# Transposes on the DMA queue in place of TensorE, in a two-group stream step

## The chip, the cores and the metric

One core of a Trainium2 chip runs the whole program. The metric is device time in microseconds of one execution, the median of three runs. TensorE (PE) multiplies, VectorE (DVE) and ScalarE (ACT) work element by element, GpSimd (POOL) and SyncE (SP) mostly start transfers, which 16 DMA engines carry out.

## The reference

One layer of an encoder for 256 prompt positions and 64 sample positions (320 columns in all, T), width 2048, float32.

```python
proj = rmsnorm(x, norm_mix) @ w_in           # q | k | v | u | vs | gates
# attention, 8 heads of 128; for the sample positions 256 cached keys and values stand ahead
z = (q @ k.T) * 128 ** -0.5
log_stay = where(mask, log_sigmoid(-z), 0)
log_rest = reverse_cumsum(log_stay) - log_stay
w = where(mask, exp(log_sigmoid(z) + log_rest), 0)
a = w @ v
# gating, 8 groups of 128 channels, chunks of 128 positions
u, vs = gelu(u), rmsnorm(gelu(vs), sgu_norm)
bb = u * (w_spatial_masked @ vs + b_spatial)
merged = sigmoid(g_a) * (a @ w_branch_a) + sigmoid(g_b) * (bb @ w_branch_b)
h = x + merged @ w_out
h = h + (silu(hn @ w_gate) * (hn @ w_up)) @ w_down     # hn = rmsnorm(h, norm_ffn), 5632 wide
y = rmsnorm(h, norm_final)
```

Outputs are y, k, v and the normalised vs rows of the sample.

## The kernel before

Features lie on the 128 partitions, the 320 positions along the free dimension. Nearly all work is projections: `block` multiplies one 128-column block of a weight with an activation in 16 chunks, in two half-blocks of 8. For each half-block `weights` loads 512 KB on SP's queue into a ring of three (`wraw`, tag `raw`), ScalarE rounds it to `wh` (line 75), VectorE takes the difference `wl` (line 76), both in rings of four (`wsplit`), and TensorE runs three matmuls a chunk (lines 83 to 85). A half-block is a tick: after each, `tick` emits what `at(tick, fn, ...)` has put there. So the attention and the gating branch lie between half-blocks of the projections of later heads. The framework's scheduler decides how each engine's instructions stand from this order and the dependencies; transfers under `keep_in_program_order` keep theirs.

Attention goes by pairs of heads (p = 0 to 3). `head_out` puts q, k, v into SBUF. `att_scores` multiplies q and k on TensorE and computes the weights on VectorE and ScalarE: `z[0]` and `z[1]` hold in the end the exponentials for the prompt (three 128 x 128 blocks a head), `z[0]` also two blocks for the cached rows, `wown` the sample's own block. `att_turn` transposes them and the values on TensorE, through `aux` banks of PSUM, from which ScalarE and VectorE copy to `wt` and `av`; `att_out` multiplies. `att_keys` and `att_rows` load cached keys and values (`cv`, one buffer). For each pair of gating groups `sgu_gain` scales `vs` (the sample's rows to `vown`), `sgu_turn` transposes five blocks on TensorE, `sgu_mix` multiplies with `wst` and `wso`. A transpose there is a matmul with the identity, `ident`.

`pair(name)` takes a 128 x 640 float32 buffer from a ring of eight, tag "D". After the branches follow the gates with the merge, the output projection and the feed-forward network, from about 330 us to the end; they are projections alone.

Of the kernel before, what the change touches and what calls it, by code (L numbers as in the profile page):

```python
# [8 lines left out]
F32 = mybir.dt.float32  # L9
# [4 lines left out]
P = 128  # L14
TP = 256
TS = 64
T = TP + TS
D = 2048
KD = D // P
H = 8  # L20
# [13 lines left out]
def stream_step(ctx: ExitStack, tc: tile.TileContext, xT, w_in, w_a, w_b, w_out, w_gu, w_down,  # L34
                gains, ws_t, bs, ck_t, cv, y_t, k_t, v_t, sv_t):
    nc = tc.nc
# [21 lines left out]
    def at(tick, fn, *a):  # L58
        assert tick > state["tick"], (tick, state["tick"])
        later.setdefault(tick, []).append((fn, a))  # L60
# [41 lines left out]
    def pair(name):  # L102
        return big.tile([P, 2 * T], F32, tag="D", bufs=8, name=name)
# [36 lines left out]
    ident = const.tile([P, P], F32, name="ident")  # L140
# [142 lines left out]
    attn = {}  # L283
    att_ctx = ExitStack()
    apool = att_ctx.enter_context(tc.tile_pool(name="attn", bufs=1))
# [21 lines left out]
    Z, KT = 384, T + PAST  # L307
# [7 lines left out]
    wown = apool.tile([P, P], F32, name="wown")  # L315
    nc.gpsimd.memset(wown, 0.0)
    ROWS = (slice(0, TS), slice(TS, P))
# [3 lines left out]
    def att_new(p):  # L321
        attn[p] = {"q": apool.tile([P, 2, T], F32, tag="q", bufs=2, name="q"),
                   "k": apool.tile([P, 2, KT], F32, tag="k", bufs=2, name="k"),
                   "v": apool.tile([P, 2, T], F32, tag="v", bufs=2, name="v"),
                   "vo": apool.tile([P, P], F32, tag="vo", name="vo")}

    def att_keys(p):
        tc.keep_in_program_order(nc.sync.dma_start(
# [44 lines left out]
        for r in ROWS:  # L373
            nc.scalar.activation(out=wown[r, r], in_=z[1][r, Z:], func=AF.Exp)

    def att_turn(p):

        s = attn[p]
        z, v = s["z"], s["v"]
        ba, bb, bs_, bv = aux(), aux(), aux(), aux()  # L380
        cols = lambda t, i: t[:, i * P : (i + 1) * P]
        for i in range(4):
            nc.tensor.transpose(cols(bv, i), v[:, i // 2, i % 2 * P : (i % 2 + 1) * P], ident)  # L383
        nc.tensor.transpose(cols(ba, 3), s["vo"], ident)
        for j, b in enumerate((ba, bb)):
            for i in range(3):
                nc.tensor.transpose(cols(b, i), cols(z[j], i), ident)  # L387
        for i in range(2):
            nc.tensor.transpose(cols(bs_, i), cols(z[0], 3 + i), ident)
        nc.tensor.transpose(cols(bs_, 2), wown, ident)  # L390
        wt = s["wt"] = apool.tile([P, 3 * Z], F32, tag="wt", name="wt")
        av = s["av"] = apool.tile([P, 5 * P], F32, tag="av", name="av")
        nc.scalar.copy(out=av[:, 0 : 4 * P], in_=bv)
        nc.vector.tensor_copy(wt[:, 0:Z], ba[:, 0:Z])
        nc.vector.tensor_copy(av[:, 4 * P :], ba[:, Z:])
        nc.scalar.copy(out=wt[:, Z : 2 * Z], in_=bb[:, 0:Z])
        nc.scalar.copy(out=wt[:, 2 * Z :], in_=bs_[:, 0:Z])

    def att_out(p):
        s = attn.pop(p)  # L400
        wt, av, cvt = s["wt"], s["av"], s["cv"]
        po = aux1(), aux()
        mm = lambda out, a, b, first, last: nc.tensor.matmul(out, a, b, start=first, stop=last, skip_group_check=True)  # L403

        mm(po[0][:, TP : TP + P], av[:, 4 * P :], wt[:, 2 * Z + 2 * P :], True, False)
        for j, r in enumerate(ROWS):
            for i in range(2):
                lo = 2 * Z + i * P + j * TS
                mm(po[0][:, TP + j * TS : TP + (j + 1) * TS], cvt[:, i, j, :], wt[:, lo : lo + TS], False, i == 1)
        for j in range(2):  # L410
            mm(po[j][:, 0:TP], av[:, 2 * j * P : (2 * j + 1) * P], wt[:, j * Z : j * Z + TP], True, False)
            mm(po[j][:, P:TP], av[:, (2 * j + 1) * P : (2 * j + 2) * P], wt[:, j * Z + TP : (j + 1) * Z], False, True)
        aT[2 * p] = split("B", po[0][:, 0:T])
        hi, lo = aT[2 * p + 1] = slot("B"), slot("B")
        for r, src in ((slice(0, TP), po[1][:, 0:TP]), (slice(TP, T), po[0][:, T : T + TS])):
            nc.scalar.copy(out=hi[:, r], in_=src)
            nc.vector.tensor_tensor(out=lo[:, r], in0=src, in1=hi[:, r].bitcast(F32), op=ALU.subtract)
# [3 lines left out]
    def head_out(name, ps, h):  # L421
        s = attn[h // 2]
        o = s[name][:, h % 2, 0:T]
        if name == "q":
            nc.vector.scalar_tensor_tensor(out=o, in0=ps, scalar=QSCALE, in1=got["rx"],
                                           op0=ALU.mult, op1=ALU.mult)
        else:
            nc.vector.tensor_tensor(out=o, in0=ps, in1=got["rx"], op=ALU.mult)
            nc.gpsimd.dma_start(out=(k_t if name == "k" else v_t)[h], in_=o)
        if name == "v":  # L430
            nc.gpsimd.tensor_copy(s["vo"][:, ROWS[h % 2]], o[:, TP:T])

    def first_out():
        for name, b in (("q", 0), ("k", 1), ("v", 2)):
# [2 lines left out]

    def attend(p, now):
        at(now + 2, att_scores, p)
        at(now + 4, att_rows, p)  # L440
        at(now + 10, att_turn, p)
        at(now + 14, att_out, p)

    att_new(0)
    at(state["tick"] + 1, first_out)
# [15 lines left out]
    vs, _ = halves(H, "vs")  # L461
    for g in range(H):
        ps = block(w_in[4 * H + g], xs)
        t = t320("ev")
# [3 lines left out]

    us, _ = halves(H, "us")
    bT: dict[int, tuple] = {}  # L470
    vown, vnat = {}, {}

    def sgu_norm():
        got["rv"] = rms("rv", [sq.total], H * P)
        sgu_gain(0)

    def sgu_gain(p):

        own = vown[p] = apool.tile([P, 2, T], F32, tag="q", bufs=2, name="vown")[:, 0, 0:P]
        for j in range(2):  # L480
            g = 2 * p + j
            for out, r in ((vs[g][:, 0:TP], slice(0, TP)), (own[:, j * TS : (j + 1) * TS], slice(TP, T))):
                nc.vector.scalar_tensor_tensor(out=out, in0=vs[g][:, r], scalar=g_sgu[:, g : g + 1],
                                               in1=got["rv"][:, r], op0=ALU.mult, op1=ALU.mult)
            nc.gpsimd.dma_start(out=sv_t[g], in_=own[:, j * TS : (j + 1) * TS])

    def sgu_turn(p):
        pt, po = aux(), aux()
        for i in range(4):
            nc.tensor.transpose(pt[:, i * P : (i + 1) * P], vs[2 * p + i // 2][:, i % 2 * P : (i % 2 + 1) * P], ident)  # L490
        nc.tensor.transpose(po[:, 0:P], vown.pop(p), ident)
        t = apool.tile([P, 5 * P], F32, tag="av", name="vsn") if p % 2 else apool.tile([P, 3 * Z], F32, tag="wt", name="vsn")
        vn = vnat[p] = t[:, 0 : 5 * P].rearrange("p (i d) -> p i d", i=5)
        nc.scalar.copy(out=vn[:, 0:4].rearrange("p i d -> p (i d)"), in_=pt)
        nc.scalar.copy(out=vn[:, 4], in_=po[:, 0:P])
        if p + 1 < H // 2:
            sgu_gain(p + 1)

    def sgu_mix(p):
        vn = vnat.pop(p)  # L500
        pg = [aux(), aux()]

        nc.tensor.matmul(pg[0][:, 256:384], vn[:, 4], wso[:, p], start=True, stop=True)
        for i in range(4):
            nc.tensor.matmul(pg[i // 2][:, i % 2 * P : (i % 2 + 1) * P], vn[:, i], wst[:, 2 * p + i // 2, :],  # L505
                             start=True, stop=True)
        for j in range(2):
            g = 2 * p + j
            b = t320("bb")
            nc.vector.tensor_tensor(out=b[:, 0:TP].rearrange("p (i t) -> p i t", i=2),  # L510
                                    in0=pg[j][:, 0:TP].rearrange("p (i t) -> p i t", i=2),
                                    in1=bsb[:, g : g + 1, :].broadcast_to([P, 2, P]), op=ALU.add)
            nc.vector.tensor_tensor(out=b[:, TP:T], in0=pg[0][:, TP + j * TS : TP + (j + 1) * TS],
                                    in1=bsb[:, g, 0:TS], op=ALU.add)
            nc.vector.tensor_tensor(out=b, in0=b, in1=us[g], op=ALU.mult)
            bT[g] = split("B", b)

    def sgu_both(p):
        if p:
            sgu_mix(p - 1)  # L520
        if p < H // 2:
            sgu_turn(p)

    base = state["tick"]
    at(base + 1, sgu_norm)
    for p in range(H // 2 + 1):
        at(base + 4 * p + 2 + (p == 0), sgu_both, p)
    for g in range(H):
        ps = block(w_in[3 * H + g], xs)
        t = t320("ev")  # L530
# [6 lines left out]
    for m in range(KD):  # L537
        gate = []
        for i in range(2):
            ps = block(w_in[5 * H + i * KD + m], xs)  # L540
            t = t320("ev")
# [8 lines left out]
        t = t320("mg", 1)  # L550
# [5 lines left out]
        lo = mpool.tile([P, T], F32R, tag="C", bufs=32, name="ml")  # L556
# [72 lines left out]
    ms, r = (const.tile([P, 3], F32, name=f"col{i}") for i in range(2))  # L629
# [9 lines left out]
    for n in (1, 1, 2, 2, 2, 2, 2, 2, 1, 1):  # L639
        y = ypair[done // 2].rearrange("p (c t) -> p c t", c=2)[:, done % 2 : done % 2 + n, :]  # L640
# [57 lines left out]
```

## Time and profile before

| what | value |
|---|---|
| runs | 1717.07, 1718.59, 1718.68 us, median 1718.59 |
| profiled execution | 1716.78 us, its span 1715.0 us |
| granted TensorE clock | 0.998 |
| busy: PE, DVE, ACT, POOL | 1702.2, 861.9, 658.8, 46.1 us |
| DMA | 263.32 MB, mean 154 GB/s |
| from 60 to 330 us (both branches) | DVE 150.6, ACT 133.6 us busy of 270, DMA share 0.46 |

The span is the time between the first and the last instruction on the core; the rest of the execution, 1.8 us, lies around it. Durations of matmuls in the profile overlap, since they are pipelined: what one costs is read from the starts of those that follow each other.

### The profile page before, as it was taken

Reading aid. Unit: us, or ns where it says so; the run is one execution under the profiler, and the core shown is the slowest. Engines: PE = TensorE matmul, PEld = TensorE weight load, DVE = VectorE, ACT = ScalarE, POOL = GpSimd, SP = SyncE. Lnnn points to the kernel's source line nnn. Section 1 sums busy time; section 2 is a strip of 40 time slices with the busy share of each in tenths; the row PEclk is TensorE's granted clock in tenths of the full one; section 3 lists DMA queues with packets and bytes.
Section 4 is the critical chain, followed back from the end, with each engine's and each line's share of the span. In section 5 each row is a group of like instructions: output and inputs, shape, how many; then the busy total and the mean of one; then the engine's idle time right before and its main releaser. Section 6 shows DMA issues by size and latency. Waiting matters only on the chain.

```text
span 1715.0 us, 27450 instructions
## 1 busy us (share of the span) xinstructions
PE 1702.2 (99%) x11616; PEld 1696.7 (99%) x11616; DVE 861.9 (50%) x1097; ACT 658.8 (38%) x819; POOL 46.1 (3%) x73
## 2 busy tenths in 40 slices
PE   9999999999999999999999999999999999999997
PEld 9999999999999999999999999999999999999997
DVE  7655446544444445555444444444444444444454
ACT  6454454433333333444333332233333323333332
POOL 0100011000000000110000000000000000000000
PEclk9999999999999999999999999999999999999999
DMA  7554444444444445554444445444444444444453
GB/s 260 162 193 143 144 154 145 139 148 148 149 153 152 148 152 165 174 171 149 150 148 148 150 152 153 148 148 148 152 151 152 148 148 150 151 153 149 130 150 114
DMA packets 80331, 263.32 MB, mean 154 GB/s; under 512 B 9008, under 2 KB 15408, under 8 KB 80208
## 3 DMA queue, kind: packets, MB, share of 16 engines
q1 hardware_dynamic: 78704, 258.25, 46.6%
q0 software_dynamic: 1088, 3.02, 0.5%
q8 instruction: 91, 1.49, 0.3%
q10 hardware_dynamic: 416, 0.31, 0.1%
q14 instruction: 32, 0.26, 0.0%
HBM read 256.03 MB, written 5.51 MB: 152 GB/s over the span
## 4 chain that ended last, share of the span: by engine, by line
issue 54%; PE 45%; DVE 0%; DMA 0%; ACT 0%; POOL 0%; POOLq 0%; ACTq 0%; DVEq 0%
PE acc L83 13%; PE acc L84 13%; PE acc L85 13%; PE aux L219 2%; PE acc L219 1%; PE aux L403 1%; DVE h L637 0%; DMA raw<-w_in 0%; PE aux L505 0%; PE aux L343 0%; PE aux L345 0%; PE aux L387 0%; PE aux L342 0%; PE aux L490 0%; PE aux L383 0%
## 5 line engine op out<-in xcount | busy, mean ns | idle before, releaser
L75 ACT CAST wh<-raw 128x1024 fp32r<-128x1024 f32 x468 | 484.5, 1036 | 988.0 <-PE acc L84 796.3
L76 DVE TENSOR_TENSOR wl<-raw,wh 128x1024 fp32r<-128x1024 f32 x468 | 564.2, 1206 | 506.4 <-ACT wh L75 503.9
L83 PE MATMUL acc<-A,wh 128*128 128x320 f32 x2464 | 763.1, 310 | 0.0
L85 PE MATMUL acc<-A,wl 128*128 128x320 f32 x2464 | 761.5, 309 | 0.0
L84 PE MATMUL acc<-A,wh 128*128 128x320 f32 x2464 | 761.4, 309 | 0.0
L83 PEld LDWEIGHTS acc<-A,wh 128*128 128x128 f32 x2464 | 462.6, 188 | 2.1 <-issue 2.0
L84 PEld LDWEIGHTS acc<-A,wh 128*128 128x128 f32 x2464 | 462.6, 188 | 0.2
L85 PEld LDWEIGHTS acc<-A,wl 128*128 128x128 f32 x2464 | 462.6, 188 | 0.0
L85 PE MATMUL acc<-B,wl 128*128 128x320 f32 x960 | 296.6, 309 | 0.0
L83 PE MATMUL acc<-B,wh 128*128 128x320 f32 x960 | 296.6, 309 | 0.0
L84 PE MATMUL acc<-B,wh 128*128 128x320 f32 x960 | 296.6, 309 | 0.0
L83 PEld LDWEIGHTS acc<-B,wh 128*128 128x128 f32 x960 | 180.2, 188 | 0.0
L84 PEld LDWEIGHTS acc<-B,wh 128*128 128x128 f32 x960 | 180.2, 188 | 0.0
L85 PEld LDWEIGHTS acc<-B,wl 128*128 128x128 f32 x960 | 180.2, 188 | 0.0
L83 PE MATMUL acc<-mh,wh 128*128 128x320 f32 x256 | 79.1, 309 | 0.0
L84 PE MATMUL acc<-ml,wh 128*128 128x320 f32 x256 | 79.1, 309 | 0.0
L85 PE MATMUL acc<-mh,wl 128*128 128x320 f32 x256 | 79.1, 309 | 0.0
L597 DVE TENSOR_TENSOR bb<-acc,rh 128x320 f32<-128x320 f32 x44 | 21.6, 491 | 57.8 <-PE acc L85 57.8
L594 DVE TENSOR_TENSOR ev<-acc,rh 128x320 f32<-128x320 f32 x44 | 21.6, 491 | 56.4 <-PE acc L85 56.3
L83 PEld LDWEIGHTS acc<-mh,wh 128*128 128x128 f32 x256 | 48.0, 188 | 0.0
L84 PEld LDWEIGHTS acc<-ml,wh 128*128 128x128 f32 x256 | 48.0, 188 | 0.0
L85 PEld LDWEIGHTS acc<-mh,wl 128*128 128x128 f32 x256 | 48.0, 188 | 0.0
(173 smaller groups left out, 696.2 us busy)
## 6 DMA issues: line engine op xcount, KB each, us to landing
raw<-w_gu SPq DMA_DIRECT2D x176, 512.0 KB, 3.5
raw<-w_in SPq DMA_DIRECT2D x141, 512.0 KB, 3.6
raw<-w_down SPq DMA_DIRECT2D x80, 512.0 KB, 3.5
raw<-w_out SPq DMA_DIRECT2D x32, 512.0 KB, 3.6
raw<-w_a SPq DMA_DIRECT2D x16, 512.0 KB, 3.5
raw<-w_b SPq DMA_DIRECT2D x16, 512.0 KB, 3.5
raw<-w_down SPq DMA_DIRECT2D x16, 256.0 KB, 2.7
xr<-xT SPq DMA_DIRECT2D x16, 160.0 KB, 2.6
```

What stands on the lines that cost most here:

```text
L75: nc.scalar.copy(out=wh[:, : n * P], in_=raw[:, : n * P])
L76: nc.vector.tensor_tensor(out=wl[:, : n * P], in0=raw[:, : n * P], in1=wh[:, : n * P].bitcast(F32), op=ALU.subtract)
L83: nc.tensor.matmul(ps[:, :T], a, x[0], start=first, stop=False)
L84: nc.tensor.matmul(ps[:, :T], a, x[1], start=False, stop=False)
L85: nc.tensor.matmul(ps[:, :T], b, x[0], start=False, stop=last)
L219: nc.tensor.matmul(first[b][h][:, :T], w[:, (h * n + j) * P : (h * n + j + 1) * P], xs[c + j][i], start=not last and c + j + i == 0, stop= ...
L403: mm = lambda out, a, b, first, last: nc.tensor.matmul(out, a, b, start=first, stop=last, skip_group_check=True)
L594: nc.vector.tensor_tensor(out=t, in0=pg, in1=got["rh"], op=ALU.mult)
L597: nc.vector.tensor_tensor(out=u, in0=pu, in1=got["rh"], op=ALU.mult)
```

## The change

The 32-bit words to be transposed are taken apart into two planes of 16 bits on ScalarE (`apart`, line 334), the low halves in one plane and the high halves in the other. One transposing DMA on SP's queue turns all 128 x 128 blocks of both planes (`turn`, line 340), and VectorE joins them to words again (`together`, line 345). This replaces the identity matmuls of `att_turn` and `sgu_turn` with their copies out of PSUM. Per pair of heads there are three such DMAs: the values (`vp`, 10 blocks of 16 bits), and the weights in two (`wp`, 10 and 8 blocks); per pair of gating groups one (`vsp`, 10 blocks). GpSimd's copies of `vo` go. The ticks move: `att_rows` from 4 to 11 after the pair's start, the turns to 6 and 12, the joins to 8 and 14, `att_out` from 14 to 16; in the gating branch each pair has a tick of its own for gain, turn, join and mix.

```diff
-                   "vo": apool.tile([P, P], F32, tag="vo", name="vo")}
+    def planes(name, n):
+        return pair(name)[:, 0:n].bitcast(U16).rearrange("p (w n) -> p n w", w=2)
+
+    def apart(to, src):
+        nc.scalar.copy(out=to, in_=src.bitcast(U16).rearrange("p (n w) -> p n w", w=2))
+
+    def turn(src):
+        n = src.shape[1]
+        to = planes("turned", n)
+        flat = lambda t: t.rearrange("p n w -> p w n").rearrange("p w n -> p (w n)")
+        tc.keep_in_program_order(nc.sync.dma_start(
+            out=flat(to).rearrange("p (b r) -> p b r", r=P), in_=flat(src), transpose=True))
+        return to
+
+    def together(to, src):
+        nc.vector.tensor_copy(to.bitcast(U16).rearrange("p (n w) -> p w n", w=2), src.rearrange("p n w -> p w n"))
...
+        y = s["wp"] = planes("wp0", 5 * P), planes("wp1", 4 * P)
+        apart(y[0], z[0])
+        apart(y[1][:, 0:Z], z[1][:, 0:Z])
+        apart(y[1][:, Z:], wown)
+    def att_turn(p, what):
         s = attn[p]
-        for i in range(4):
-            nc.tensor.transpose(cols(bv, i), v[:, i // 2, i % 2 * P : (i % 2 + 1) * P], ident)
-        nc.tensor.transpose(cols(ba, 3), s["vo"], ident)
-        for j, b in enumerate((ba, bb)):
-            for i in range(3):
-                nc.tensor.transpose(cols(b, i), cols(z[j], i), ident)
-        for i in range(2):
-            nc.tensor.transpose(cols(bs_, i), cols(z[0], 3 + i), ident)
-        nc.tensor.transpose(cols(bs_, 2), wown, ident)
...
+        s[what] = [turn(t) for t in ((s["vp"],) if what == "vt" else s["wp"])]
+
+    def att_join(p, what):
+        s = attn[p]
+        t = s[what]
+        if what == "vt":
+            av = s["av"] = apool.tile([P, 5 * P], F32, tag="av", name="av")
+            together(av, t[0])
+        else:
+            wt = s["wt"] = apool.tile([P, 9 * P], F32, tag="wt", name="wt")
+            together(wt[:, 0 : 5 * P], t[0])
+            together(wt[:, 5 * P :], t[1])
...
         if name == "v":
-            nc.gpsimd.tensor_copy(s["vo"][:, ROWS[h % 2]], o[:, TP:T])
+            j = h % 2
+            if j == 0:
+                s["vp"] = planes("vp", 5 * P)
+            apart(s["vp"][:, j * TP : (j + 1) * TP], o[:, 0:TP])
+            apart(s["vp"][:, 4 * P + j * TS : 4 * P + (j + 1) * TS], o[:, TP:T])
...
         at(now + 2, att_scores, p)
-        at(now + 4, att_rows, p)
-        at(now + 10, att_turn, p)
-        at(now + 14, att_out, p)
+        at(now + 6, att_turn, p, "vt")
+        at(now + 11, att_rows, p)
+        at(now + 8, att_join, p, "vt")
+        at(now + 12, att_turn, p, "wt")
+        at(now + 14, att_join, p, "wt")
+        at(now + 16, att_out, p)
...
     def sgu_turn(p):
-        pt, po = aux(), aux()
-        for i in range(4):
-            nc.tensor.transpose(pt[:, i * P : (i + 1) * P], vs[2 * p + i // 2][:, i % 2 * P : (i % 2 + 1) * P], ident)
-        nc.tensor.transpose(po[:, 0:P], vown.pop(p), ident)
...
+        vturned[p] = turn(vplane.pop(p))
...
-    for p in range(H // 2 + 1):
-        at(base + 4 * p + 2 + (p == 0), sgu_both, p)
+    for p, mix in enumerate((9, 11, 14, 18)):
+        at(base + 1 + 3 * p, sgu_gain, p)
+        at(base + 6 + 3 * p, sgu_turn, p)
+        at(base + (8, 10, 13, 16)[p], sgu_join, p)
+        at(base + mix, sgu_mix, p)
```

How the order moves is shown for pair 1 of the heads. First SP's queue, before: weight loads (`raw`) with the cached rows and keys of pairs 1 and 2 between them.

```order
L70 DMA raw<-w_in 128x1024 x5
L334 DMA cv<-cv 128x2x256
L70 DMA raw<-w_in 128x1024 x2
L328 DMA k<-ck_t 128x2x256
L70 DMA raw<-w_in 128x1024 x9
```

The same place after:

```order
L70 DMA raw<-w_in 128x1024 x6
L340 DMA_TRANSPOSE turned<-vp 128x10x128
L70 DMA raw<-w_in 128x1024
L354 DMA cv<-cv 128x2x256
L348 DMA k<-ck_t 128x2x256
L70 DMA raw<-w_in 128x1024
L340 DMA_TRANSPOSE turned<-wp_1186 128x10x128
L340 DMA_TRANSPOSE turned<-wp_1187 128x8x128
L70 DMA raw<-w_in 128x1024 x10
```

Three transposing DMAs have come in among the loads, with two loads between the first and the second. Each weight load waits for the split three half-blocks before it. Now VectorE, shortly after its last operation on the weights of pair 1, before (`wl` are the weight splits, `q`, `k`, `v` the heads of pair 2):

```order
L76 TENSOR_TENSOR wl<-raw,wh 128x1024 x2
L428 TENSOR_TENSOR v<-acc,rx 128x320
L76 TENSOR_TENSOR wl<-raw,wh 128x1024 x2
L428 TENSOR_TENSOR k<-acc,rx 128x320
L76 TENSOR_TENSOR wl<-raw,wh 128x1024 x2
L425 SCALAR_TENSOR_TENSOR q<-acc,rx 128x320
L76 TENSOR_TENSOR wl<-raw,wh 128x1024
L394 COPY wt<-aux 128x384
L395 COPY av<-aux 128x128
L76 TENSOR_TENSOR wl<-raw,wh 128x1024
```

The same after, where `B` are the results of pair 0:

```order
L76 TENSOR_TENSOR wl<-raw,wh 128x1024 x3
L448 TENSOR_TENSOR v<-acc,rx 128x320
L76 TENSOR_TENSOR wl<-raw,wh 128x1024
L118 TENSOR_TENSOR B<-aux_1320,B 128x320
L437 TENSOR_TENSOR B<-aux,B 128x256
L437 TENSOR_TENSOR B<-aux_1320,B 128x64
L345 COPY av<-turned 128x2x640
L76 TENSOR_TENSOR wl<-raw,wh 128x1024
L345 COPY wt<-turned 128x2x640
L345 COPY wt<-turned 128x2x512
L448 TENSOR_TENSOR k<-acc,rx 128x320
L76 TENSOR_TENSOR wl<-raw,wh 128x1024 x2
```

The copies out of PSUM, behind eight splits of weights, have become three joins behind four and five, and each join stands ahead of the splits that follow.

On ScalarE the words of `wp` are taken apart right after the exponentials of pair 1:

```order
L75 CAST wh<-raw 128x1024 x2
L392 ACT_TABLE_LOAD
L392 ACTIVATE z_1157<-z_1157 128x384
L394 ACTIVATE wown<-z_1157 64x64 x2
L391 ACTIVATE z_1156<-z_1156 128x640
L334 COPY wp_1186<-z_1156 128x640x2
L334 COPY wp_1187<-z_1157 128x384x2
L334 COPY wp_1187<-wown 128x128x2
L75 CAST wh<-raw 128x1024 x2
L334 COPY vp<-v 128x256x2
```

These three copies of `wp` now stand ahead of the next two casts of weights.

More of the change, by code (lines that the diff above doesn't have):

```diff
@@ L323, in att_new @@
                    "k": apool.tile([P, 2, KT], F32, tag="k", bufs=2, name="k"),
-                   "v": apool.tile([P, 2, T], F32, tag="v", bufs=2, name="v"),
-                   "vo": apool.tile([P, P], F32, tag="vo", name="vo")}
+                   "v": apool.tile([P, 2, T], F32, tag="v", bufs=2, name="v")}
+    U16 = mybir.dt.uint16
+    def planes(name, n):
[11 more added lines that the diff above has]
+        nc.vector.tensor_copy(to.bitcast(U16).rearrange("p (n w) -> p w n", w=2), src.rearrange("p n w -> p w n"))
     def att_keys(p):
@@ L374, in att_scores @@
             nc.scalar.activation(out=wown[r, r], in_=z[1][r, Z:], func=AF.Exp)
-    def att_turn(p):
-        s = attn[p]
-        z, v = s["z"], s["v"]
-        ba, bb, bs_, bv = aux(), aux(), aux(), aux()
-        cols = lambda t, i: t[:, i * P : (i + 1) * P]
-        for i in range(4):
-            nc.tensor.transpose(cols(bv, i), v[:, i // 2, i % 2 * P : (i % 2 + 1) * P], ident)
-        nc.tensor.transpose(cols(ba, 3), s["vo"], ident)
-        for j, b in enumerate((ba, bb)):
-            for i in range(3):
-                nc.tensor.transpose(cols(b, i), cols(z[j], i), ident)
-        for i in range(2):
[L389 to L397, printed above, removed]
+        y = s["wp"] = planes("wp0", 5 * P), planes("wp1", 4 * P)
[3 more added lines that the diff above has]
+    def att_turn(p, what):
+        s = attn[p]
+        s[what] = [turn(t) for t in ((s["vp"],) if what == "vt" else s["wp"])]
[9 more added lines that the diff above has]
+            together(wt[:, 5 * P :], t[1])
     def att_out(p):
@@ L403, in att_out @@
         mm = lambda out, a, b, first, last: nc.tensor.matmul(out, a, b, start=first, stop=last, skip_group_check=True)
-        mm(po[0][:, TP : TP + P], av[:, 4 * P :], wt[:, 2 * Z + 2 * P :], True, False)
+        mm(po[0][:, TP : TP + P], av[:, 4 * P :], wt[:, 8 * P :], True, False)
         for j, r in enumerate(ROWS):
             for i in range(2):
-                lo = 2 * Z + i * P + j * TS
+                lo = Z + i * P + j * TS
                 mm(po[0][:, TP + j * TS : TP + (j + 1) * TS], cvt[:, i, j, :], wt[:, lo : lo + TS], False, i == 1)
         for j in range(2):
-            mm(po[j][:, 0:TP], av[:, 2 * j * P : (2 * j + 1) * P], wt[:, j * Z : j * Z + TP], True, False)
-            mm(po[j][:, P:TP], av[:, (2 * j + 1) * P : (2 * j + 2) * P], wt[:, j * Z + TP : (j + 1) * Z], False, True)
+            w = wt[:, j * 5 * P : j * 5 * P + Z]
+            mm(po[j][:, 0:TP], av[:, 2 * j * P : (2 * j + 1) * P], w[:, 0:TP], True, False)
+            mm(po[j][:, P:TP], av[:, (2 * j + 1) * P : (2 * j + 2) * P], w[:, TP:], False, True)
         aT[2 * p] = split("B", po[0][:, 0:T])
@@ L470, in stream_step @@
     bT: dict[int, tuple] = {}
-    vown, vnat = {}, {}
+    vplane, vturned, vnat = {}, {}, {}
     def sgu_norm():
         got["rv"] = rms("rv", [sq.total], H * P)
-        sgu_gain(0)
     def sgu_gain(p):
-        own = vown[p] = apool.tile([P, 2, T], F32, tag="q", bufs=2, name="vown")[:, 0, 0:P]
+        own = apool.tile([P, 2, T], F32, tag="q", bufs=2, name="vown")[:, 0, 0:P]
         for j in range(2):
@@ L485, in sgu_gain, with sgu_join @@
             nc.gpsimd.dma_start(out=sv_t[g], in_=own[:, j * TS : (j + 1) * TS])
+        y = vplane[p] = planes("vsp", 5 * P)
+        for j in range(2):
+            apart(y[:, j * TP : (j + 1) * TP], vs[2 * p + j][:, 0:TP])
+        apart(y[:, 4 * P :], own)
     def sgu_turn(p):
-        pt, po = aux(), aux()
-        for i in range(4):
[L490 to L497, printed above, removed]
+        vturned[p] = turn(vplane.pop(p))
+    def sgu_join(p):
+        t = apool.tile([P, 5 * P], F32, tag="av", name="vsn") if p % 2 else apool.tile([P, 9 * P], F32, tag="wt", name="vsn")
+        together(t[:, 0 : 5 * P], vturned.pop(p))
+        vnat[p] = t[:, 0 : 5 * P].rearrange("p (i d) -> p i d", i=5)
     def sgu_mix(p):
@@ L516, in sgu_mix @@
             bT[g] = split("B", b)
[L518 to L522, printed above, removed]
     base = state["tick"]
     at(base + 1, sgu_norm)
-    for p in range(H // 2 + 1):
-        at(base + 4 * p + 2 + (p == 0), sgu_both, p)
+    for p, mix in enumerate((9, 11, 14, 18)):
[3 more added lines that the diff above has]
+        at(base + mix, sgu_mix, p)
     for g in range(H):
```

## The prediction

> **What bounds the kernel now.** The page's busy table, the clock row, the shares of the chain that ended last, and the DMA queues came first.
>
> ```profile
> span 1715.0 us, 27450 instructions
> PE 1702.2 (99%) x11616; PEld 1696.7 (99%) x11616; DVE 861.9 (50%) x1097; ACT 658.8 (38%) x819; POOL 46.1 (3%) x73
> PEclk9999999999999999999999999999999999999999
> issue 54%; PE 45%; DVE 0%; DMA 0%; ACT 0%; POOL 0%; POOLq 0%; ACTq 0%; DVEq 0%
> q1 hardware_dynamic: 78704, 258.25, 46.6%
> q10 hardware_dynamic: 416, 0.31, 0.1%
> ```
>
> TensorE has no holes at full clock, so each of its instructions taken away is time saved, as long as no wait takes its place. Every other engine and the DMA have half their time free. Next I read the timeline of TensorE at one turn of the attention (pair 0) and one of the gating branch.
>
> ```profile
> 87.75 0.31 PE L85 MATMUL acc<-A,wl 128*128 128x320 f32 x1
> ...
> 93.03 0.31 PE L85 MATMUL acc<-A,wl 128*128 128x320 f32 x1
> 93.18 0.60 PE L383 MATMUL aux<-ident,v 128*128 128x128 f32 x4
> 93.61 0.27 PE L384 MATMUL aux<-ident,vo 128*128 128x128 f32 x1
> 93.72 0.82 PE L387 MATMUL aux<-ident,z 128*128 128x128 f32 x6
> 94.38 0.38 PE L389 MATMUL aux<-ident,z 128*128 128x128 f32 x2
> 94.59 0.27 PE L390 MATMUL aux<-ident,wown 128*128 128x128 f32 x1
> 94.62 0.39 PE L83 MATMUL acc<-A,wh 128*128 128x320 f32 x1
> 94.85 0.31 PE L84 MATMUL acc<-A,wh 128*128 128x320 f32 x1
> 95.00 0.31 PE L85 MATMUL acc<-A,wl 128*128 128x320 f32 x1
> ...
> 279.67 0.60 PE L490 MATMUL aux<-ident,vs 128*128 128x128 f32 x4
> 280.11 0.27 PE L491 MATMUL aux<-ident,vown 128*128 128x128 f32 x1
> 280.13 0.39 PE L83 MATMUL acc<-A,wh 128*128 128x320 f32 x1
> 280.36 0.31 PE L84 MATMUL acc<-A,wh 128*128 128x320 f32 x1
> ```
>
> 36 projection matmuls start between 87.75 and 93.03, so one costs 0.147 us and a half-block (8 x 3 of them) 3.52 us. This is the tick of the order.
>
> **What goes.** From the L85 at 93.03 to that at 95.00 are 1.97 us; three matmuls explain 0.44, so 14 transposes cost 1.53 us, far less than their durations added. Four pairs: 6.1 us. In the gating branch, 279.67 to 280.36 is 0.69 us, less one matmul 0.54 us; four: 2.2 us. The products L403 and L505 stay. TensorE loses **8.3 us**. GpSimd's copies of `vo` are off the chain and count nothing.
>
> **What ScalarE and VectorE get.**
>
> ```profile
> L393 ACT COPY av<-aux 128x512 f32<-128x512 f32 x4 | 2.3, 578 | 0.0
> L397 ACT COPY wt<-aux 128x384 f32<-128x384 f32 x4 | 2.0, 492 | 0.0
> L396 ACT COPY wt<-aux 128x384 f32<-128x384 f32 x4 | 1.9, 480 | 0.0
> L359 ACT ACTIVATE e<-e 128x640 f32<-128x640 f32 x4 | 3.0, 739 | 0.0
> L359 ACT ACTIVATE e<-e 128x448 f32<-128x448 f32 x4 | 2.3, 563 | 0.0
> L495 ACT COPY vsn<-aux 128x128 f32<-128x128 f32 x4 | 1.1, 272 | 0.0
> L416 ACT CAST B<-aux 128x256 fp32r<-128x256 f32 x4 | 1.5, 373 | 0.7 <-PE aux L403 0.7
> L394 DVE COPY wt<-aux 128x384 f32<-128x384 f32 x4 | 2.2, 550 | 0.0
> L395 DVE COPY av<-aux 128x128 f32<-128x128 f32 x4 | 1.1, 280 | 0.0
> ```
>
> A word cut in two counts as two elements. ScalarE: 739 - 563 over 192 elements is 0.92 ns each, so `wp` costs 1.33 + 0.86 + 0.37 = 2.6 us a pair, the four `vp` copies 2 x (0.58 + 0.27) = 1.7; it loses 1.55. VectorE: (550 - 280)/256 is 1.05 ns, so a join of 1280 elements costs 1.5 us, of 1024 1.2: 4.2 a pair against 0.83 removed. A gating pair costs ScalarE some 1.6 and VectorE 1.5 us. These prices are not measured for 16-bit elements at a stride of two; from half (if 16-bit runs faster) to double is their range. Both engines have half their time free, but they also split the weights, and there the order matters, as follows.
>
> **Where TensorE has little in reserve.** VectorE and ScalarE around the scores of pair 1 (timeline before):
>
> ```profile
> 101.79 1.05 ACT L75 CAST wh<-raw 128x1024 fp32r<-128x1024 f32 x1 [2.47 <-PE acc L84]
> ...
> 103.14 1.22 DVE L76 TENSOR_TENSOR wl<-raw,wh 128x1024 fp32r<-128x1024 f32 x1
> 109.76 1.36 DVE L360 SCALAR_TENSOR_TENSOR e<-z,e 128x640 f32<-128x640 f32 x2 [4.42 <-ACT e L359]
> 116.42 1.22 DVE L76 TENSOR_TENSOR wl<-raw,wh 128x1024 fp32r<-128x1024 f32 x1
> 117.68 2.35 DVE L76 TENSOR_TENSOR wl<-raw,wh 128x1024 fp32r<-128x1024 f32 x2
> 122.81 1.22 DVE L76 TENSOR_TENSOR wl<-raw,wh 128x1024 fp32r<-128x1024 f32 x1 [1.62 <-ACT wh L75]
> 127.67 0.49 DVE L428 TENSOR_TENSOR k<-acc,rx 128x320 f32<-128x320 f32 x1 [0.25 <-PE acc L85]
> ```
>
> No weight is split from 104.4 to 116.4. The cast at 101.79 waited for TensorE to free the oldest of four buffers, so its split, at 103.14, is the fourth half-block ahead: TensorE has two blocks to go through. The block after these ends at 127.6 (row of `k`), began two ticks earlier, at 120.5, and needs the split done at 117.64: a reserve of 2.9 us. The next are done at 118.9, 120.0 and 124.0 and needed at 124.0, 127.5 and 131.0: reserves of 5.1, 7.5 and 7.0 us. In the new order ScalarE makes `wp` in just this gap (2.6 us, of 2.9), and VectorE meets the joins four and five splits later. By then some 7 us less 2.6 and less the first join's 1.5 is about **3 us per pair for all waiting**; beyond it TensorE stands.
>
> **How long the joins wait.** SP issues a pair's `vp` after the load that the first split behind the scores releases (a ring of three), `wp` after that of the third. The first join stands behind the fourth split after the scores, the second and third behind the fifth. Between third split and second join VectorE has two splits (2.4), one `v` (0.5), three `B` (1.1) and a join (1.5): 5.5 us of cover, much the same for `vp`. A transfer waits its turn behind the load just issued. What it takes no row shows; the nearest:
>
> ```profile
> y_t<-h SPq DMA_DIRECT2D x6, 320.0 KB, 2.3
> raw<-w_in SPq DMA_DIRECT2D x141, 512.0 KB, 3.6
> sv_t<-vown POOLq DMA_DIRECT2D x8, 32.0 KB, 2.0
> ```
>
> About 2.0 us is fixed (32 KB). The load ahead adds 1.6 (3.6 less the fixed part). Call X the transfer of one 128 x 1280 block of 16 bits (328 KB; the second `wp`, with 1024, is priced alike). Lower bound, by bytes: 46.6% of 16 x 1715 us over 258.25 MB gives 328 KB in **1.0 us**. Upper bound, by pieces: a transposed row is 256 bytes, 1280 rows, 80 per DMA engine; the same share over 78,704 packets is 162 ns for 3.3 KB, so **13 us** if a row costs a whole packet. Between: the other queue's 0.1% over 416 packets is 66 ns for 0.75 KB, which with the first point leaves 38 ns plus 0.038 ns a byte, 47 ns a row, **3.8 us** (rounding alone allows 33 to 99 ns for the 66). I take 1.0 to 2.5: the plain 320 KB of `y_t` land in 2.3 us, and the 256-byte rows of `sv_t` in no more than the fixed time. The Trainium skill bears on this in Advanced Engine Details and Errata, X-Bar Transpose (TRN2): transposing DMAs run about as fast as plain ones, 350 to 400 GB/s, which would make X an estimated 0.8 to 0.9 us.
>
> A pair waits (1.6 + 2.0 + X - 5.5) twice, for `vp` and the first `wp`, and X - 1.5 for the second, queued behind: 3X - 5.3 us, of which 3 are free. Above X = 2.8 the time is 8.3 us saved less 4 x (3X - 8.3); TensorE breaks even at X = 3.5. The gating turns are left out: their splits have the usual reserve of two to three ticks. How long SP itself is held by an issue is not shown; it mostly stands waiting for split buffers, so some microseconds are free. Moving `cv` later takes it off a wait for the previous pair's product and costs nothing. Products come two ticks later in the order; nothing on TensorE reads them before the merge.
>
> **Sum.** The profiled execution took 1716.78 us, 1.8 under the median shown. 1716.8 - 8.3 = 1708.5; at the median **1710.3**. No change means here within 0.2%, 3.4 us.
>
> **Rivals.**
>
> *Rows at 47 ns, X = 3.8 or more.* The joins wait 6.1 us a pair, 3.1 too many, and the weight splits behind them are late: 12.4 - 8.3 = +4, **1723 us**; at X = 6 it is +30. For it speaks the two-point fit, against it that both points read or write main memory. It decides from X = 3.5 on. It ends slower.
>
> *Rows at a packet's price, X = 13.* Waits of 33.7 us a pair, 30.7 uncovered: 4 x 30.7 - 8.3 = +115, **1833 us**, with the gating turns some more. The queue would be over-full too: 39 us of transposes beside 47% of the 49 us of a pair. Nothing in the profile excludes it. The Trainium skill, VectorE: DVE Perf Modes, The three transpose paths, gives 1309 ns for one 128 x 128 block of 16 bits on the DMA path and 390 on TensorE, and advises TensorE where its output may go to PSUM; ten blocks one after another would be an estimated 13.1 us. That page speaks against this change.
>
> *The lean spot alone eats the gain.* If 16-bit copies cost twice (5.2 us of `wp` in a reserve of 2.9, joins of 3 us), each pair stalls about 2 us: 4 x 2 = 8 of the 8.3 back, **1718 us**. For it: both are strided. The same result comes from X of 3.2 to 3.7.
>
> **How the numbers follow.** The forecast (X up to 3.1 and copies near their price): 0.48. No change: 0.13. Rows near 47 ns, up to X = 6 or so: 0.20. Far slower: 0.19. The range goes from 1708.5 (the whole gain, in a run as fast as the fastest shown, 1717.07) to X = 6, 1750; the forecast's own range is 1708.5 to 1715. Faster 0.48, same 0.13, slower 0.39.
>
> **What would show it.** Right: no identity transposes in the groups of TensorE, its rows without holes from 60 to 330 us, a transpose landing in under 5 us, the joins with idle time of a few tenths. Wrong: rows of L85 that wait for `wl` of VectorE behind a join, joins that wait for `turned`, casts that wait for `raw`, and a DMA share near one in this stretch; then packets of 256 bytes tell which price held.

## The result, and the profile after

The changed kernel takes **1742.26 us** (median of 4 runs, 1740.42 to 1744.04) against 1718.59 before: a ratio of 1.0142, interval 1.013 to 1.0155, so 1.4% slower, 32 us above the forecast. The profiled execution took 1744.04 us for a span of 1742.3.

The busy table, the DMA lines and the shares of the chain, from the page after:

```profile
span 1742.3 us, 27337 instructions
PE 1708.6 (98%) x11540; PEld 1699.8 (98%) x11540; DVE 868.3 (50%) x1105; ACT 736.4 (42%) x838; POOL 42.6 (2%) x65
DMA packets 100299, 268.30 MB, mean 154 GB/s; under 512 B 28976, under 2 KB 35376, under 8 KB 100176
q1 hardware_dynamic: 98672, 263.23, 48.0%
issue 54%; PE 38%; ACT 4%; DVE 3%; DMA 1%; POOL 0%; POOLq 0%; ACTq 0%; DVEq 0%; SPq 0%
```

TensorE has 76 instructions fewer, as foreseen, yet it is busy longer, over a longer span. ScalarE, which was no part of the chain, is now 4% of it; the transposes take the transfers' share on DMA queue 1 from 46.6% only to 48.0%. Next, the groups of ScalarE's new copies and one of VectorE's joins, between 50 and 360 us (busy time, mean ns of one, idle time ahead of them):

```profile
L334 ACT COPY wp<-z 128x1280 uint16<-128x1280 uint16 x4 | 24.2, 6062 | 0.1
L334 ACT COPY vp<-v 128x512 uint16<-128x512 uint16 x8 | 20.9, 2609 | 2.7 <-DVE v L448 2.7
L334 ACT COPY vsp<-vs 128x512 uint16<-128x512 uint16 x8 | 20.2, 2722 | 0.0
L334 ACT COPY wp<-z 128x768 uint16<-128x768 uint16 x4 | 16.1, 4028 | 0.0
...
L334 ACT COPY wp<-wown 128x256 uint16<-128x256 uint16 x4 | 6.7, 1662 | 0.0
...
L345 DVE COPY wt<-turned 128x1280 uint16<-128x1280 uint16 x4 | 3.6, 896 | 5.0 <-DMA turned<-wp 5.0
```

The copy of 1280 elements takes 6.06 us, where the prediction had 1.33: (6062 - 1662) over 1024 elements is **4.30 ns an element**, against 0.92. VectorE's join of as many takes 0.90, less than predicted. Who waited in the two branches (some rows of the view; engine and tile, what ended the idle time, us in all, times, the longest):

```profile
PE acc L83 <- ACT wh L75: 16.8, 6, 4.6
PE acc L85 <- DVE wl L76: 4.0, 7, 0.7
DVE vsn L345 <- DMA turned<-vsp: 12.2, 3, 6.8
DVE wt L345 <- DMA turned<-wp: 5.0, 2, 3.6
DVE av L345 <- DMA turned<-vp: 4.1, 1, 4.1
```

TensorE stands 20.8 us there, all of it for weights that ScalarE has not yet cast, or VectorE not yet split. The timelines of ScalarE, VectorE and TensorE at the first pair show one such wait (start, length, the operation; in brackets the idle time before it):

```profile
81.94 9.60 ACT L334 COPY wp<-z 128x1280 uint16<-128x1280 uint16 x2
91.02 1.65 ACT L334 COPY wp<-wown 128x256 uint16<-128x256 uint16 x1
92.17 3.31 ACT L334 COPY vp<-v 128x512 uint16<-128x512 uint16 x2
94.99 3.23 ACT L75 CAST wh<-raw 128x1024 fp32r<-128x1024 f32 x3
```

```profile
83.28 0.49 DVE L448 TENSOR_TENSOR k<-acc,rx 128x320 f32<-128x320 f32 x1
96.37 1.23 DVE L76 TENSOR_TENSOR wl<-raw,wh 128x1024 fp32r<-128x1024 f32 x1 [12.60 <-ACT wh L75]
```

```profile
91.34 0.31 PE L84 MATMUL acc<-A,wh 128*128 128x320 f32 x1
91.49 0.31 PE L85 MATMUL acc<-A,wl 128*128 128x320 f32 x1
96.39 0.64 PE L83 MATMUL acc<-A,wh 128*128 128x320 f32 x1 [4.59 <-ACT wh L75]
96.82 0.47 PE L84 MATMUL acc<-A,wh 128*128 128x320 f32 x1
97.65 0.64 PE L85 MATMUL acc<-A,wl 128*128 128x320 f32 x1 [0.36 <-DVE wl L76]
98.08 0.47 PE L83 MATMUL acc<-A,wh 128*128 128x320 f32 x1
98.35 0.47 PE L84 MATMUL acc<-A,wh 128*128 128x320 f32 x1
...
102.80 0.31 PE L83 MATMUL acc<-A,wh 128*128 128x320 f32 x1
102.94 0.31 PE L84 MATMUL acc<-A,wh 128*128 128x320 f32 x1
```

From 81.94 ScalarE does nothing for 13 us but take words apart; its next cast starts at 94.99, VectorE idles 12.6 us ahead of the split, and TensorE runs dry at 91.8. What follows is a second loss: after the wait the matmuls start 0.267 us apart (98.08 to 98.35), and only from 102.8 again 0.14. The windows of this stretch, of a later quiet one, and of the whole stage show it in the granted clock (stretch and its length, then busy PE, PEld, DVE, ACT, POOL with their counts, the clock, the DMA share and GB/s; the last row is the whole stage in the kernel before):

```profile
90.00:95.00 5.00, 1.80 (x13) 1.53 (x11) 0.00 (x0) 5.00 (x5) 0.00 (x0) 1.00 0.63 115
95.00:100.00 5.00, 3.25 (x11) 2.85 (x12) 3.63 (x5) 3.22 (x4) 0.82 (x1) 0.58 0.62 194
100.00:110.00 10.00, 10.00 (x62) 10.00 (x62) 6.16 (x7) 6.08 (x5) 0.54 (x1) 0.87 0.84 283
150.00:180.00 30.00, 30.00 (x205) 29.03 (x204) 17.79 (x31) 21.44 (x25) 1.08 (x2) 1.00 0.47 149
60.00:340.00 280.00, 259.23 (x1681) 251.45 (x1681) 146.28 (x227) 200.73 (x195) 17.88 (x27) 0.96 0.55 154
...
60.00:340.00 280.00, 280.00 (x1933) 275.89 (x1932) 155.84 (x244) 137.57 (x192) 21.50 (x33) 1.00 0.46 150
```

The clock falls to 0.58 behind the wait and is 1.00 where there was none. From 60 to 340 us TensorE is idle for 20.8 us, where the kernel before has no idle time at all.

### The profile page after: what moved, and what is told of

It reads as the page before. It is cut to its first block, busy times and chain, and to the rows that moved or that the text cites. A ratio compares the mean times of both kernels' runs of the same rounds, so it can differ in the third digit from the quotient of the medians.

```text
span 1742.3 us, 27337 instructions
## 1 busy us (share of the span) xinstructions
PE 1708.6 (98%) x11540; PEld 1699.8 (98%) x11540; DVE 868.3 (50%) x1105; ACT 736.4 (42%) x838; POOL 42.6 (2%) x65
## 2 busy tenths in 40 slices
DMA packets 100299, 268.30 MB, mean 154 GB/s; under 512 B 28976, under 2 KB 35376, under 8 KB 100176
## 4 chain that ended last, share of the span: by engine, by line
issue 54%; PE 38%; ACT 4%; DVE 3%; DMA 1%; POOL 0%; POOLq 0%; ACTq 0%; DVEq 0%; SPq 0%
PE acc L85 11%; PE acc L84 11%; PE acc L83 11%; PE aux L219 2%; ACT wp L334 1%; PE acc L219 1%; DVE wl L76 1%; ACT vsp L334 1%; DMA raw<-w_in 1%; DVE e L387 0%; DMA turned<-wp 0%; DVE h L660 0%; ACT wh L75 0%; DVE e L380 0%; ACT e L377 0%
```

## The experiments

Unless said otherwise, a kernel differs from the changed one by the lines shown, and was compared with the kernel before on the same chip (1718.5 to 1718.7 us there). Ratios are to the kernel before. A kernel of one run has no interval. Where whole words are copied (e3, e7, e9) the buffers are also taken as 32-bit words, and the transposing DMA reads them as the same 16-bit elements; those lines are not shown.

**e1: the two planes one after the other.** In the change the copy writes a word's low half into the first plane, its high half into the second, and so on, back and forth; here it writes one whole plane, then the other (and so reads every second half, instead of half after half). The same elements land in the same places.

```
-        nc.scalar.copy(out=to, in_=src.bitcast(U16).rearrange("p (n w) -> p n w", w=2))
+        nc.scalar.copy(out=to.rearrange("p n w -> p w n"), in_=src.bitcast(U16).rearrange("p (n w) -> p w n", w=2))
```

> Only the order in which ScalarE walks through a word copy changes: all low halves first, then all high halves, so that it writes each plane in one run instead of jumping between the planes with every element. Theory A (the jumping writes of single 16-bit elements make the copy slow): a copy of 1280 elements falls from 6.06 us to 1.3 or so, the casts of weights are no longer late, and the whole gain of 8 us over the kernel before appears: about 1710 us. Theory B (any 16-bit element costs ScalarE 4.3 ns): 6.06 us as now and 1742 us.

Measured: **1710.38 us** (1709.9 to 1710.92), ratio 0.9952, interval 0.9937 to 0.9967. Groups between 50 and 360 us, then waits:

```profile
L334 ACT COPY wp<-z 128x1280 uint16<-128x1280 uint16 x4 | 5.0, 1260 | 0.1
...
L334 ACT COPY vp<-v 128x512 uint16<-128x512 uint16 x8 | 4.9, 617 | 2.4 <-DVE v L448 2.4
```

```profile
DVE wt L345 <- DMA turned<-wp: 10.9, 6, 3.3
DVE av L345 <- DMA turned<-vp: 8.3, 3, 4.2
DVE vsn L345 <- DMA turned<-vsp: 5.4, 3, 3.2
```

The one line makes the copy 4.8 times as fast and the kernel as fast as forecast. The joins now wait 24.6 us for the transposes, more than in the slow kernel, and TensorE waits for no weight in this stage. So the whole loss hangs on the order in which these copies go through their elements; e6 tells reading from writing.

**e2: the same order, on VectorE.**

```
-        nc.scalar.copy(out=to, in_=src.bitcast(U16).rearrange("p (n w) -> p n w", w=2))
+        nc.vector.tensor_copy(to.rearrange("p n w -> p w n"), src.bitcast(U16).rearrange("p (n w) -> p w n", w=2))
```

> The words are taken apart on VectorE, plane by plane, ScalarE does nothing for it. A 1280-element copy should cost VectorE what its join costs, 0.9 us. Theory (the loss comes from ScalarE's copies, behind which its casts of weights wait): about 1710 us, 8 under the kernel before. Rival (the transposing DMAs and the joins that wait for them cost it): the casts are early and the time stays well above 1718, up to 1740.

Measured: 1709.99 us (1708.74 to 1710.86), ratio 0.9949, interval 0.9934 to 0.9964; a copy of 1280 elements takes 0.819 us. The engine doesn't matter once the order is right.

**e3: whole words copied.** The copies move 32-bit words, in order, so no word is cut. They are multiplied by zero on the way, so what attention and the gating branch contribute is left out of the result.

```
-        nc.scalar.copy(out=to, in_=src.bitcast(U16).rearrange("p (n w) -> p n w", w=2))
+        nc.scalar.activation(out=to, in_=src, func=AF.Copy, scale=0.0)
```

> ScalarE copies whole 32-bit words (times zero) to the place of the planes, half the elements and none of 16 bits; the same DMAs turn them and the same joins follow. The result leaves out the attention and the gating. It separates the DMA from the copies: by the theory (copies alone) 1708 to 1711 us; by the rival (transposes landing in 5.5 us make the joins late) 1720 us or more, with TensorE waiting for wl behind a join.

Measured: 1710.18 us (1709.83 to 1710.43), ratio 0.995, interval 0.9936 to 0.9965. 640 words take 0.740 us, 0.59 of what the 1280 halves take in e1, yet the kernel gains nothing by it: at the price of e1 ScalarE's part is already hidden.

**e4: no transposing DMA.** The joins read the planes directly; values, weights and gate rows reach their products untransposed. All the rest is the changed kernel, slow copies included.

```
     def turn(src):
-        n = src.shape[1]
...
-        return to
+        return src
```

> The transposing DMAs are left out, the joins read the planes as ScalarE made them; the products get untransposed operands. ScalarE's copies stay as slow as they are. By the theory that these copies cost the time: still 1738 to 1742 us, since only the joins' 21 us of waiting for turned go, and these lie under the wait for the casts. By the rival (the DMA costs it): 1710 us.

Measured: 1742.47 us (1740.73 to 1743.72), ratio 1.0135, interval 1.0118 to 1.0152: as slow as with the transposes. Waits of e4:

```profile
PE acc L83 <- ACT wh L75: 16.0, 6, 4.6
PE acc L85 <- DVE wl L76: 3.9, 7, 0.8
```

TensorE's waits stay where they were. The DMA transposes cost this kernel nothing that can be measured.

**e5: the change's back-and-forth order, on VectorE** (one run).

```
-        nc.scalar.copy(out=to, in_=src.bitcast(U16).rearrange("p (n w) -> p n w", w=2))
+        nc.vector.tensor_copy(to, src.bitcast(U16).rearrange("p (n w) -> p n w", w=2))
```

> VectorE takes the words apart with the order of the change: it jumps between the two planes with every 16-bit element. If jumping writes are what costs, whatever the engine, a 1280-element copy takes about 6 us in place of the 0.82 it took plane by plane, and the time rises far above 1742 us (some 85 us of copies on the engine that splits the weights). If it is ScalarE's own weakness: 0.8 to 1.4 us a copy and 1710 us.

Measured: 1720.0 us.

```profile
L334 DVE COPY wp<-z 128x1280 uint16<-128x1280 uint16 x4 | 12.3, 3084 | 0.0
...
L334 DVE COPY wp<-wown 128x256 uint16<-128x256 uint16 x4 | 4.0, 1004 | 0.0
```

Neither of the two expected outcomes came. (3084 - 1004)/1024 is 2.03 ns an element, where e2's rows, 819 and 285 ns, give 0.52: 3.9 times. The order is dear on both engines, on ScalarE more so; the price is not one that the memory sets alike for both. TensorE now waits 6.0 us in all for `wl` (6 times).

**e6: jumping reads instead of jumping writes** (one run). e1, and the join made by ScalarE, reading the two planes back and forth and writing in order.

```
-        nc.vector.tensor_copy(to.bitcast(U16).rearrange("p (n w) -> p w n", w=2), src.rearrange("p n w -> p w n"))
+        nc.scalar.copy(out=to.bitcast(U16).rearrange("p (n w) -> p n w", w=2), in_=src)
```

> Words are taken apart plane by plane, as in the mended order, and the join moves to ScalarE, where it reads jumping between the planes and writes word after word. If the jumping writes alone cost: a join of 1280 takes 1.3 us and the time is 1710 us. If rows of two elements cost, read or written: about 6 us a join and 1800 us or more.

Measured: 1709.05 us.

```profile
L345 ACT COPY wt<-turned 128x1280 uint16<-128x1280 uint16 x4 | 5.7, 1418 | 7.4 <-DMA turned<-wp 7.3
```

1.42 us for 1280 elements read back and forth, against 1.26 for e1's plane by plane: reading this way is nearly free. The dear part is the writing.

**e7: 32-bit words written back and forth** (one run) between the two halves of the tile, again times zero (attention and gating left out of the result, as in e3).

```
-        nc.scalar.copy(out=to, in_=src.bitcast(U16).rearrange("p (n w) -> p n w", w=2))
+        nc.scalar.activation(out=to.rearrange("p (h i) -> p i h", h=2), in_=src.rearrange("p (i h) -> p i h", h=2),
+                             func=AF.Copy, scale=0.0)
```

> As with whole words copied (times zero, so attention and gating are left out of the result), but ScalarE writes 32-bit words jumping between the two halves of the place. If jumping costs for any size, 4.3 ns a word: 640 words take 2.8 us in place of 0.74, and the time lies between 1711 and 1722 us. If it is the 16-bit element that costs when written out of line: 0.74 us and 1710 us.

Measured: 1710.9 us.

```profile
L337 ACT ACTIVATE wp<-z 128x640 f32<-128x640 f32 x4 | 5.6, 1402 | 0.1
...
L337 ACT ACTIVATE wp<-wown 128x128 f32<-128x128 f32 x4 | 1.8, 438 | 0.0
```

The copy lies between the two expected prices. (1402 - 438)/512 is 1.88 ns a word, against 0.87 in order ((740 - 295)/512 in e3). Jumping costs whole words too, but 2.2 times, where halves cost 5.1 times (4.30 against 0.84 ns, the latter from e1's 1260 and 402). Why a half costs more than a word no run tells.

**e8: only the gating copies keep the change's order**; the attention's are those of e1 (that line is not shown again).

```
+    def apart_jump(to, src):
         nc.scalar.copy(out=to, in_=src.bitcast(U16).rearrange("p (n w) -> p n w", w=2))
...
-            apart(y[:, j * TP : (j + 1) * TP], vs[2 * p + j][:, 0:TP])
-        apart(y[:, 4 * P :], own)
+            apart_jump(y[:, j * TP : (j + 1) * TP], vs[2 * p + j][:, 0:TP])
+        apart_jump(y[:, 4 * P :], own)
```

> Only the gating branch keeps the jumping copies, the attention has them plane by plane. ScalarE then has 27 us of slow copies instead of 88. By the waits of TensorE for casts in the changed kernel, which lie near 91, 136, 185, 240 us in the attention and near 302 and 313 to 319 in the gating branch, about a quarter to a third of the 32 us between the two orders should come back: 1718 to 1722 us. If a single slow stretch already cost most of it: above 1730.

Measured: 1720.17 us (1718.15 to 1720.87, 10 runs), ratio 1.0006, interval 0.9997 to 1.0016. TensorE waits 4.0 us for `wh` and 1.4 for `wl`. Of the 32 us between e1 and the changed kernel, 10 come from the four gating turns (9.8 over e1) and by difference 22 from the four pairs. That is 31% of the loss, from 26% of the time of the slow copies: by the groups of the changed kernel, most of them shown above, these last 103 us in all (the expectation had 88), 27 of them in the gating branch.

**e9: how far the jump must be** (one run). The attention's copies write back and forth between two neighbouring blocks of `d` elements each, so `d` is the distance of a jump in 16-bit elements. They read with the same jumps; e6 found those nearly free. The pairs' first `wp` have d = 2, 8, 64 and 640, the heads' first `vp` 2, 4, 8 and on to 256. Words times zero as in e3; attention and gating are left out of the result.

```
+    def apart_far(to, src, d):
+        nc.scalar.activation(out=to.bitcast(U16).rearrange("p (a w b) -> p a b w", w=2, b=d),
+                             in_=src.bitcast(U16).rearrange("p (a b w) -> p a b w", w=2, b=d),
+                             func=AF.Copy, scale=0.0)
...
+        apart_far(y[0], z[0], (2, 8, 64, 640)[p])
...
+            apart_far(s["vp"][:, j * TP : (j + 1) * TP], o[:, 0:TP], 2 << h)
```

> Whole words times zero (attention and gating are left out of the result), but the copies of the first weight plane and of the values write their 16-bit elements alternating between two places that lie d elements apart: d is 2, 8, 64, 640 for the weights of pairs 0 to 3 (1280 elements) and 2, 4, 8, 16, 32, 64, 128, 256 for the values of heads 0 to 7 (512 elements). If leaving a line of 16 bytes is what costs (the Trainium skill, SBUF, speaks of such lines), d of 2 and 4 are near 1.3 and 0.6 us and from d of 8 on all cost the same 6.0 and 2.6 us. If distance as such costs, the time rises with d throughout. If each out-of-order element costs, d of 2 is already at 6.0 and 2.6.

Measured: 1713.62 us. ScalarE's timeline, in order of time (heads 0 and 1, pair 0, heads 2 and 3, and pairs 1 and 3):

```profile
54.37 0.63 ACT L340 ACTIVATE vp<-v 128x512 uint16<-128x512 uint16 x1 [0.42 <-DVE v L456]
55.06 0.61 ACT L340 ACTIVATE vp<-v 128x512 uint16<-128x512 uint16 x1
80.52 1.27 ACT L340 ACTIVATE wp<-z 128x1280 uint16<-128x1280 uint16 x1
82.31 2.50 ACT L340 ACTIVATE vp<-v 128x512 uint16<-128x512 uint16 x1
100.17 2.55 ACT L340 ACTIVATE vp<-v 128x512 uint16<-128x512 uint16 x1 [0.43 <-DVE v L456]
119.03 6.03 ACT L340 ACTIVATE wp<-z 128x1280 uint16<-128x1280 uint16 x1
...
213.34 6.08 ACT L340 ACTIVATE wp<-z 128x1280 uint16<-128x1280 uint16 x1
```

A jump of 2 or 4 elements (4 or 8 bytes) costs nothing: 0.63 and 0.61 us, as e1's 0.62. From 8 elements (16 bytes) on the whole price is there, 2.50 us, and it does not grow: 6.03 us at 16 bytes, 6.08 at 1280. A step between 8 and 16 bytes and a flat line behind it fit a memory that is written in lines of 16 bytes, where leaving a line with every element costs. The Trainium skill, Advanced Engine Details and Errata, SBUF Cachelines, states just that line size, and a penalty where each access goes to another line; it gives no size of it and does not tell writes from reads, and by e6 reads hardly pay here.

**e10: e1 again, in more rounds**, as the version that beats both kernels.

> The kernel that takes the words apart plane by plane, again, for the interval: 1710 us, 0.9952 of the kernel before, with TensorE's rows free of waits from 60 to 340 us.

Measured: **1710.85 us** (1709.94 to 1711.5), ratio 0.9958, interval 0.9944 to 0.9971.

**e11: halves written at every second place** (one run). e1 with the join on ScalarE, plane by plane: it writes 16-bit halves four bytes apart, so no word is written whole, but lines are passed in order.

```
-        nc.vector.tensor_copy(to.bitcast(U16).rearrange("p (n w) -> p w n", w=2), src.rearrange("p n w -> p w n"))
+        nc.scalar.copy(out=to.bitcast(U16).rearrange("p (n w) -> p w n", w=2), in_=src.rearrange("p n w -> p w n"))
```

> Words taken apart plane by plane, and ScalarE also joins them plane by plane: it writes single 16-bit elements at a step of two, first all low halves, then all high halves, never jumping back. If a write of half a word costs as such, a join of 1280 takes about 6 us and the time exceeds 1800 us. If only the jumping costs: 1.3 to 1.4 us, as where it read jumping, and 1709 to 1711 us.

Measured: 1709.44 us; such a join of 1280 elements takes 1.656 us, 1.3 times e1's 1.260, not 4.8 times. Writing half-words with gaps is thus cheap where four in a row fall into 16 bytes. But lines of 16 bytes with one price for each change of line do not explain all. Against e1 this join changes its line once more in eight elements, for 0.31 ns an element (1656 less 1361 ns for 256 elements is 1.15, less 0.84), so 2.5 ns a change; the change's copies do it seven times more in eight, for 3.46 ns an element, so 4.0 a change. Whether coming back to a line just left costs extra was not tried by itself.

## Why the prediction was wrong, step by step

**What goes: right.** With the copies mended the kernel gains 8.1 us (1718.52 to 1710.38) in e1 and 7.7 (1718.5 to 1710.85) in e10, of 8.3 predicted. The forecast of 1710.3 is the time of e1, not of the change.

**What ScalarE gets: the step that failed.** The prediction counted a word cut in two as two elements of 0.92 ns and gave half to double as the range. In e1's order that price is right within a tenth (1.26 + 0.83 + 0.40 = 2.5 us a pair against 2.6), in the change's it is 4.30 ns, 6.06 + 4.03 + 1.66 = **11.75 us a pair**. The output access pattern, `to` as "p n w" over planes that lie apart, stood in the diff; every row the price was taken from wrote in order. The prediction allowed a factor of two for the stride, and did not ask what the order of writing could cost.

**The lean spot: the wrong reserve.** The pairs wait behind the `wp` copies, and the rival on the lean spot named the mechanism. But 2.9 us is the reserve of the first split after the scores, and the copies do not hold that one up: in the order on ScalarE shown with the change two casts stand ahead of them (in the first pair three), so the late split is the third, for which the prediction itself had 7.5 us. The changed kernel's trace agrees: from the first copy to the next cast ScalarE takes 13.1, 10.2, 10.2 and 13.6 us in the four pairs (the recorded durations, 11.75 in sum, overlap a little; in the first pair copies of `vp` lie there too, in the last some work of the gating branch), and TensorE then stands 5.0, 1.1, 3.1 and 4.5 us in two waits each. That leaves a reserve of 7.1 to 9.1 us. Accordingly 7.2 us of `wp` copies a pair in e9 (6.06 + 0.85 + 0.30, in three of four pairs) left TensorE waiting 3.1 us in all, and the kernel at 1713.62, where the rival had 1718 for 5.2 us. The prediction's own sum with the measured price, waits of 11.75 - 2.9 = 8.9 us and so 4 x 8.9 less 8.3, would have given 1745.9. It is near the measured time by luck: the pairs wait some 14 us in place of 35.6, and nothing stands there for the clock or for the gating turns, which were left out and which e8 puts at 10 us.

**What a wait costs: missing.** e1's span is 33.6 us shorter than the changed kernel's (1708.7 against 1742.3). Idle TensorE is 20.8 of these. Between 50 and 350 us 76 projection matmuls more than in e1, behind the waits, started some 0.267 us after the one ahead instead of 0.147; together that is another 9 us. The rest, about 4, lies in the steps right around each wait, where starts lie 0.25 to 0.43 us apart, idle time taken off. So here each us of waiting cost 1.6. The prediction priced waits at their length, and that is right where the clock stays up: e9's row of the same stage has 3.2 us of idle TensorE at a clock of 1.00, and its span is 3.1 us above e1's (1711.8 against 1708.7).

```profile
60.00:340.00 280.00, 276.84 (x1882) 271.32 (x1881) 164.46 (x255) 168.31 (x209) 17.55 (x27) 1.00 0.60 171
```

**VectorE's joins: cheaper than predicted**, 0.90 and 0.75 us against 1.5 and 1.2.

**The transposes: the feared cost did not come.** X, the transfer, was taken as 1.0 to 2.5 us, and two rivals had 3.8 and 13. In e1 the median from issue to landing is 6.8, 5.2 and 5.2 us for `wp`, `vp` and `vsp`; less the predicted 2.0 fixed and 1.6 for the load ahead, an estimate of X is 1.6 to 3.2 us, which still holds the time of the issue: each held SP for 1.3 to 3.7 us, which the prediction had left open. (The landings are longer than the 5 us that were to show the forecast right.) The pieces were nearly as the upper bound had them, 4 x (1280 + 1280 + 1024 + 1280) = 19,456 rows: the page has 19,968 packets more, and 19,968 more under 512 bytes (28,976 less 9,008). A row did not cost a whole packet, though, which would have been 13 us. And the joins' waits of e1, 19.2 us over four pairs or 4.8 a pair, more than the 3 called free, stopped no matmul: one sign of being wrong, joins that wait for `turned`, stands in the kernel that has the whole gain. And e4 shows the transposes worth nothing either way. Of the two pages of the Trainium skill weighed there, the rule of X-Bar Transpose is nearer to these landings than the 13.1 us worked out from The three transpose paths: in the changed kernel, e1 and e10 no transpose took over 9.0 us to land, load ahead included.

**The chances.** Slower had 0.39, all of it on the DMA transposes, which cost nothing; the case that came about had its mechanism inside the 0.13 for no change.

## What to carry to other kernels

Price a copy by the order in which it *writes*, and read the output access pattern innermost first: two planes or halves of a tile written in turn, element by element, 16 bytes or more apart, cost 2 to 5 times the copy that fills one after the other. Swap the two innermost loops so that the gaps fall on the reading side. Before pricing a delay of a feeder of TensorE, find which of its items comes late, and take the reserve of that one. And when the feeder is late by some microseconds, count the wait more than once where the clock falls behind it: over e1 the span grew by 1.6 times the waits in the changed kernel and in e5, by 1.9 in e8 (10.0 us for 5.4), and by 1.0 in e9, where it did not fall.

## What the runs showed of the hardware that was not expected

- A 16-bit write that goes to another place 16 or more bytes away each time: 4.30 ns on ScalarE against 0.84 in order; over 1280 bytes on VectorE 2.03 against 0.52, and for a 32-bit write on ScalarE 1.88 against 0.87. On ScalarE a jump of 4 or 8 bytes is free, and jumping reads cost 1.1 times.
- After idle stretches TensorE's granted clock was 0.58 in the five microseconds with the restart, and its matmuls were slow for some 5 us. The Trainium skill, TensorE: Matmul & The Clock Gate, part 1, has half speed after an idle window of about 3.4 us, and full speed after as long a busy one. The waits of 4.59, 3.85 and 3.76 us fit. But a single wait of 2.28 us in e5 was followed by 12 starts at half speed (at 92.07, clock 0.50 from there to 95.43), and in the changed kernel waits of 2.49 and 0.60 us, 0.7 us apart (at 187.7), by some 20. A shorter pair did so once and once not: 1.77 and 0.70 us in e8 were followed by 13 slow starts, 1.73 and 0.69 us in the changed kernel (at 303.6) by none, with a clock of 1.00. So here shorter waits were sometimes enough; what decides was not tried.
